# Residues of the matmul operands' addresses, spread over a 512-byte period, in a two-layer decoder trunk

## The chip, the cores and the metric

The kernel runs on one core of a Trainium2 chip. The metric is the device time of one execution in microseconds (us); less is better. A core has a tensor engine (PE, whose loads of the stationary operand are listed as PEld), a vector engine (DVE), a scalar engine (ACT), GpSimd (POOL) and a queue engine (SP) that starts DMAs. Operands of PE lie in the on-chip memory SBUF, 128 partitions wide; an address below is a byte offset within a partition, and its *residue* is the remainder after division by 512.

## The reference

256 tokens of width 2048 go through one layer of gated linear attention (GLA, 4 heads) and one layer of retention (8 heads), each with a SiLU gate path, and a last RMSNorm. All is float32.

```python
h = x
h = h + gla_mixer(rms_norm(h, gla_norm[0]), gla_w_in[0], gla_w_a1[0], gla_w_a2[0], gla_b_a[0], gla_head_g[0], gla_w_out[0])
h = h + retention_mixer(rms_norm(h, ret_norm[0]), positions, ret_w_in[0], ret_gn_g[0], ret_gn_b[0], ret_w_out[0])
return rms_norm(h, final_norm)
# a mixer, in short
q, k, v, gate = split(h @ w_in)                  # widths 1024/1024/4096/4096 in GLA, 2048/2048/4096/4096 in retention
o = per_head_norm(chunked_attention(q, k, v))    # with decays, scores masked causally
return (o * silu(gate)) @ w_out                  # 4096 -> 2048
```

## The kernel before

**Precision by parts.** A float32 number x is split into `hi`, what PE's "r" format of 32 bits keeps of it, and `lo` = x - `hi`. A product of tokens and weights is then three matmuls that add up in one PSUM bank: token-high by weight-hi, token-high by weight-lo, token-low by weight-hi (`mm3`, L341 to L343, and `three`, L412 to L414). The q and k projections take two and a half: the weight is the loaded operand there, 256 columns of high and 256 of low tokens stream past `hi` at once (L372, L382, L384), and the high tokens alone past `lo` (L374, L381, L385).

**Weights.** They come from HBM in pieces of 512 KB (two k-tiles of 128 rows by 512 columns, [128, 1024] in SBUF) into eight `raw` buffers, and a few into two spare ones. `emit_split` (L284 on) splits a piece: ACT copies `raw` to `hi` (L298), DVE subtracts to `lo` (L299). Pools `hi` and `lo` have four buffers each; `split_tiles` hands out a pair. `next_weights` splits up to three pieces (LOOK) ahead of the matmuls. The last pieces' `hi` parts lie in the tokens' tile, which is free by then. Some pieces are sums of two weight blocks, formed by accumulating DMAs and DVE adds (L293), for a scheme that saves matmuls by combining blocks of tokens and of weights (`pair`, `values_and_gates`, `out_pair`; the sums of tokens are the tiles `sums`, `xsum`, `osum`, `rsum`).

**Tokens.** `xhl` holds the normalised tokens, transposed: 16 k-tiles of [128, 2, 256], the 2 being high and low part. `ogt` holds the gated outputs of half the heads in the same form, for the output projection. Both are filled by ACT and DVE (L500, L501, L546, L549, L714, L715) and read by PE for most of the run: a k-tile's 128 tokens as the loaded operand against weight parts, or 512 columns of a k-tile as the streamed operand in the q and k groups. `make_sums` reads them for the sums of tokens (L448).

**Addresses.** Tiles of the pool `one` are placed one behind the other in the order of the `const` calls (rounded up to 32 bytes), and the pools `rs`, `raw`, `hi`, `lo` and the others behind them. `xhl` begins at 5,120, `ogt` at 37,888, and each `hi` and `lo` buffer at a multiple of 4,096 plus 1,024: all of residue 0, as are all k-tiles, their halves, and the two 512-column parts of a weight piece. A few small operands lie elsewhere: `ones_r` (loaded in L776) at 73,888, and the 48-column slices of `wa1` (loaded in L640) at a distance of 192 bytes.

**Order.** The work of one head (scores, norms, gate, transposes) is cut into steps of generators, `side` and `tasks`, which `advance` and `step` run between the matmuls of the next group; the framework's scheduler then orders each engine's instructions, and `keep` pins some. For every matmul PE gets a load of its stationary operand and the matmul itself; loads run while the matmul before them streams.

Of the kernel before, what the change touches and what calls it, by code (L numbers as in the profile page):

```python
# [11 lines left out]
F32R = mybir.dt.float32r  # L12
# [5 lines left out]
P = 128  # L18
SEQ = 256
D = 2048  # L20
EPS = 1e-6
NKT = D // P
GW = 512
SUB = 2
# [154 lines left out]
def kernel(  # L179
# [23 lines left out]
    hi_p = pool("hi", 4)  # L203
    lo_p = pool("lo", 4)
# [16 lines left out]
    def const(shape, name, dtype=F32):  # L221
        return one.tile(shape, dtype, tag=name, name=name)
# [51 lines left out]

    def split_tiles(i):
        if i < last0:
            hi = hi_p.tile([P, SUB, GW], F32R, tag="hi", name=f"hi{i}")
            lo = lo_p.tile([P, SUB, GW], F32R, tag="lo", name=f"lo{i}")
            return hi, lo
        j = i - last0  # L280
        hi = xhl[:, j * SUB : (j + 1) * SUB].rearrange("p k a t -> p k (a t)")
        return hi, t4_p.tile([P, SUB, GW], F32R, tag="t4", name=f"tail{j}")

    def emit_split(pieces=1, between=None):  # L284
        i = emitted["sub"]
        c, pre, post = subs[i]
        emit_raws(c)
        src = raws[c]
        for n in range(i + 1, min(i + 1 + EARLY, len(subs))):
            at, by = subs[n][:2]  # L290
            if by is not None and n not in added:
                added.add(n)
                nc.vector.tensor_tensor(raws[at], raws[at], raws[by], ALU.add)  # L293
        hi, lo = split_tiles(i)
        step = SUB // pieces
        for k in range(pieces):
            sl = slice(k * step, (k + 1) * step)
            a = nc.scalar.activation(hi[:, sl], src[:, sl], AF.Copy)  # L298
            b = nc.vector.tensor_tensor(lo[:, sl], src[:, sl], hi[:, sl].bitcast(F32), ALU.subtract)  # L299
            if i >= last0 - 4:  # L300
                keep(a)
                keep(b)
            if i == 0:
                first(a, b)
                if k == 0:
                    between()
        splits[i] = (hi, lo)
        emitted["sub"] += 1
        for n, key in post:
            nc.gpsimd.dma_start(raws[n], block(key), accum_op=ALU.add)  # L310
        emit_raws(c)
# [193 lines left out]
    sm = const([P, 96], "smalls")[:, 0:S_N]  # L505
    ident = const([P, P], "ident")
    cur["resid"] = rs_p.tile([P, 2, D], F32, tag="rs", name="resid")
    xhl = const([P, NKT, 2, SEQ], "xhl", F32R)
    ogt = const([P, NKT, 2, SEQ], "ogt", F32R)
    trig = const([P, 2, SEQ], "trig")  # L510
    rr = const([P, 2, 2], "rr")
    r2_ = const([P, 2, 2], "r2")
# [1075 lines left out]
```

## Time and profile before

| | before |
|---|---|
| median of 2 runs | 1374.33 us (1373.35 to 1375.31) |
| profiled execution: span from first to last instruction | 1371.5 us |
| PE busy, matmuls | 1362.3 us, 99%, 6,564 |
| DVE busy | 1098.4 us, 80% |
| ACT busy | 847.0 us, 62% |
| HBM read and written | 303.35 MB and 10.49 MB, 229 GB/s |
| mean granted clock of PE | 0.999 |

A profile is of one execution. A row of a group gives the kernel's line, the engine, the operation, the tile written and the tiles read, the size, the count; then the busy time in us, the mean duration of one in ns, and the engine's idle time just before, with what ended it. A row of the chain gives the start in us from the span's start, how long the piece held the chain, and what it was. A row of waits gives who waited for whom, the us in total, how often, and the longest. A row of the busy times of a stretch gives the stretch, its length, then busy us and count for PE, PEld, DVE and ACT, then the granted clock, the share of DMA time and GB/s. Matmuls overlap, so a matmul's duration (some 390 ns for 512 columns) is longer than the distance between two.

### The profile page before, as it was taken

The page shows a single profiled execution, that of the slowest core. Times are in us where ns is not written, and L with a number is a line of the kernel's source. Part 1 is how long each engine was busy: PE and PEld are TensorE (multiplying, and loading weights), DVE is VectorE, ACT ScalarE, POOL GpSimd, SP SyncE. Part 2 cuts the span into 40 slices and gives each one's busy share as a digit, 9 for nine tenths or more (in the row PEclk, how much of TensorE's full clock was granted, in tenths as well). Part 3 has the DMA queues.
Part 4 walks back from the last instruction along what each step waited for, and adds up shares of the span by engine and source line. Part 5 has one row for each costly group of instructions (what it writes and reads, how often), then busy time and mean ns, then how long its engine had stood idle before and what let it go on. Part 6 is the DMA issues. An engine that isn't in the chain of part 4 may idle for free.

```text
span 1371.5 us, 18372 instructions
## 1 busy us (share of the span) xinstructions
PE 1362.3 (99%) x6564; PEld 1145.0 (83%) x6564; DVE 1098.4 (80%) x1520; ACT 847.0 (62%) x1119; POOL 136.8 (10%) x194
## 2 busy tenths in 40 slices
PE   9999999999999999999999999999999999999997
PEld 8888888888888888888888888888888888888886
DVE  6686795987878896769887988897867897889796
ACT  6576656656567756656666576655546665666565
POOL 1003020110021021001011010100101101010010
PEclk9999999999999999999999999999999999999999
DMA  9755566789658667868897878796798797979773
GB/s 358 259 175 168 169 208 184 156 247 318 200 153 262 204 204 183 319 169 232 267 331 197 260 202 249 207 316 218 172 367 219 240 261 197 259 198 317 241 176 124
DMA packets 84508, 315.04 MB, mean 230 GB/s; under 512 B 9776, under 2 KB 10800, under 8 KB 83136
## 3 DMA queue, kind: packets, MB, share of 16 engines
q1 hardware_dynamic: 67200, 241.63, 50.4%
q0 software_dynamic: 15920, 64.89, 23.9%
q10 hardware_dynamic: 1296, 7.35, 1.4%
q8 instruction: 51, 0.84, 0.2%
q14 instruction: 41, 0.34, 0.1%
HBM read 303.35 MB, written 10.49 MB: 229 GB/s over the span
## 4 chain that ended last, share of the span: by engine, by line
PE 99%; DMA 1%; DVE 0%; ACT 0%; DVEq 0%; issue 0%; ACTq 0%
PE rqk_ps L384 8%; PE re_ps L412 8%; PE re_ps L413 8%; PE re_ps L414 8%; PE rqk_ps L385 4%; PE gqk_ps L384 4%; PE gg_ps L342 3%; PE gv_ps L343 3%; PE gv_ps L341 3%; PE gv_ps L342 3%; PE gg_ps L341 3%; PE gg_ps L343 3%; PE ge_ps L412 2%; PE ge_ps L413 2%; PE ge_ps L414 2%; PE gae_ps L413 2%
## 5 line engine op out<-in xcount | busy, mean ns | idle before, releaser
L299 DVE TENSOR_TENSOR lo<-raw,hi 128x1024 fp32r<-128x1024 f32 (+1 forms) x568 | 687.4, 1221 | 215.5 <-ACT hi L298 205.5
L298 ACT ACTIVATE hi<-raw 128x1024 fp32r<-128x1024 f32 (+1 forms) x568 | 595.9, 1055 | 394.3 <-DMA raw<-in_w_all 50.8
L384 PE MATMUL rqk_ps<-xhl,hi 128*128 128x512 f32 x480 | 162.9, 397 | 0.0
L413 PE MATMUL re_ps<-lo,xhl 128*128 128x512 f32 x352 | 137.5, 391 | 0.0
L414 PE MATMUL re_ps<-hi,xhl 128*128 128x512 f32 x352 | 137.3, 390 | 0.0
L310 POOL DMA_DIRECT2D raw<-in_w_all x90 | 78.0, 868 | 556.1 <-DVE lo L299 222.1
L412 PE MATMUL re_ps<-hi,xhl 128*128 128x512 f32 x352 | 132.6, 391 | 0.0
L385 PE MATMUL rqk_ps<-xhl,lo 128*128 128x256 f32 x480 | 122.5, 281 | 0.0
L384 PEld LDWEIGHTS rqk_ps<-xhl,hi 128*128 128x128 f32 x480 | 89.7, 188 | 17.8
L385 PEld LDWEIGHTS rqk_ps<-xhl,lo 128*128 128x128 f32 x480 | 87.6, 189 | 3.4
L414 PEld LDWEIGHTS re_ps<-hi,xhl 128*128 128x128 f32 x352 | 66.1, 188 | 13.6
L413 PEld LDWEIGHTS re_ps<-lo,xhl 128*128 128x128 f32 x352 | 66.2, 188 | 13.2
L412 PEld LDWEIGHTS re_ps<-hi,xhl 128*128 128x128 f32 x352 | 66.0, 188 | 13.2
L384 PE MATMUL gqk_ps<-xhl,hi 128*128 128x512 f32 x216 | 76.6, 399 | 0.0
L342 PE MATMUL gg_ps<-lo,xhl 128*128 128x512 f32 x192 | 75.5, 393 | 0.0
L342 PE MATMUL gv_ps<-lo,xhl 128*128 128x512 f32 x192 | 75.3, 392 | 0.0
L341 PE MATMUL gv_ps<-hi,xhl 128*128 128x512 f32 x192 | 75.2, 393 | 0.0
L343 PE MATMUL gv_ps<-hi,xhl 128*128 128x512 f32 x192 | 75.1, 391 | 0.0
L343 PE MATMUL gg_ps<-hi,xhl 128*128 128x512 f32 x192 | 75.0, 391 | 0.0
L341 PE MATMUL gg_ps<-hi,xhl 128*128 128x512 f32 x192 | 74.9, 392 | 0.0
L829 POOL TENSOR_TENSOR s<-s,m 128x64 f32<-128x64 f32 x56 | 36.1, 676 | 232.5 <-DVE m L820 223.2
L385 PE MATMUL gqk_ps<-xhl,lo 128*128 128x256 f32 x216 | 59.1, 281 | 0.0
(434 smaller groups left out, 2659.8 us busy)
## 6 DMA issues: line engine op xcount, KB each, us to landing
raw<-in_w_all SPq DMA_DIRECT2D x449, 512.0 KB, 4.9
raw<-in_w_all POOLq DMA_DIRECT2D x90, 512.0 KB, 6.8
resid<-in_x_n SPq DMA_DIRECT2D x2, 1024.0 KB, 10.8
gg<-in_gn_g POOLq DMA_DIRECT2D x8, 256.0 KB, 4.2
resid_x<-resid ACTq DMA_DIRECT2D x1, 2048.0 KB, 7.9
gb<-in_gn_b POOLq DMA_DIRECT2D x8, 256.0 KB, 6.0
gb_resid<-resid_x POOLq DMA_DIRECT2D x1, 2048.0 KB, 11.3
resid_g<-gb_resid ACTq DMA_DIRECT2D x1, 2048.0 KB, 10.5
```

Of the source, the lines that this page charges most:

```text
L298: a = nc.scalar.activation(hi[:, sl], src[:, sl], AF.Copy)
L299: b = nc.vector.tensor_tensor(lo[:, sl], src[:, sl], hi[:, sl].bitcast(F32), ALU.subtract)
L310: nc.gpsimd.dma_start(raws[n], block(key), accum_op=ALU.add)
L341: pin(mm(ps, xh, hi[:, q, :], start=kt == 0, stop=False, **onto))
L342: pin(mm(ps, xh, lo[:, q, :], start=False, stop=False, **onto))
L343: pin(mm(ps, xl, hi[:, q, :], start=False, stop=kt == end - 1, **onto))
L384: mm(ps[c], wh, rhs[:, kt, :, :], start=kt == 0, stop=False)
L385: mm(ps[c][:, 0, :], wl, rhs[:, kt, 0, :], start=False, stop=False)
L412: pin(mm(ps, xh, hi[:, q, :], start=start, stop=False, **again))
L413: pin(mm(ps, xh, lo[:, q, :], start=False, stop=False, **again))
L414: pin(mm(ps, xl, hi[:, q, :], start=False, stop=stop, **again))
L829: nc.gpsimd.tensor_tensor(dst, dst, side_of(m[:, li, :], z), ALU.add)
```

## The change

Each buffer of `hi` and `lo` becomes 64 bytes longer (16 floats), so the four buffers of a pool begin 64 bytes further on in residue each. A k-tile of `xhl` becomes 16 bytes longer and one of `ogt` 32 bytes, and an unused tile of 256 bytes stands between the two. The views that the rest of the kernel sees have the shapes of before.

```diff
     def split_tiles(i):
         if i < last0:
-            hi = hi_p.tile([P, SUB, GW], F32R, tag="hi", name=f"hi{i}")
-            lo = lo_p.tile([P, SUB, GW], F32R, tag="lo", name=f"lo{i}")
-            return hi, lo
+            both = []
+            for p, tag in ((hi_p, "hi"), (lo_p, "lo")):
+                t = p.tile([P, SUB * GW + 16], F32R, tag=tag, name=f"{tag}{i}")
+                both.append(t[:, 0 : SUB * GW].rearrange("p (k n) -> p k n", n=GW))
+            return both
...
-    xhl = const([P, NKT, 2, SEQ], "xhl", F32R)
-    ogt = const([P, NKT, 2, SEQ], "ogt", F32R)
+    rows = lambda t: t[:, :, 0 : 2 * SEQ].rearrange("p k (a t) -> p k a t", a=2)
+    xhl = rows(const([P, NKT, 2 * SEQ + 4], "xhl", F32R))
+    const([P, 64], "gap")
+    ogt = rows(const([P, NKT, 2 * SEQ + 8], "ogt", F32R))
```

## The prediction

> **What bounds the kernel now.** I read the page first (its busy times, its slices, its chain), then the waits of PE, then the chain in order of time for single stretches, then the groups by form, and last the busy times of the whole span for one tile at a time.
>
> ```profile
> span 1371.5 us, 18372 instructions
> PE 1362.3 (99%) x6564; PEld 1145.0 (83%) x6564; DVE 1098.4 (80%) x1520; ACT 847.0 (62%) x1119; POOL 136.8 (10%) x194
> DVE  6686795987878896769887988897867897889796
> PEclk9999999999999999999999999999999999999999
> PE 99%; DMA 1%; DVE 0%; ACT 0%; DVEq 0%; issue 0%; ACTq 0%
> PE warm_ps L521 <- POOL lnone L523: 1.0, 1, 1.0
> PE zps L640 <- DVE wa L614: 0.4, 1, 0.4
> ```
>
> The chain that ended last is 99% PE, the granted clock is full in every slice, and the whole list of what PE waited for is the last two rows: 1.4 us. So the time is 6,564 matmuls one behind the other, some 208 ns apart on average, plus about 9 us of start and end. DVE and ACT cost nothing while the weights they split arrive in time, and the two rows say that they do. The change moves addresses and nothing else, so what matters is the distance from the start of one matmul to the start of the next, which I call a step. The chain in order of time gives it, because each piece there lasts until the next begins (a matmul's own duration doesn't: they overlap).
>
> ```profile
> 716.87 0.23 PE re_ps L413
> ...
> 718.91 0.23 PE re_ps L414
> ...
> 746.43 0.91 PE rqk_ps L384 x4
> 747.34 0.47 PE rqk_ps L385 x4
> 747.81 0.23 PE rqk_ps L384
> 748.05 0.12 PE rqk_ps L385
> ...
> 749.23 0.94 PE rqk_ps L384 x4
> ```
>
> From the first to the second row lie nine steps of 512 columns in 2.04 us: 226.7 ns each. Four steps of 512 columns take 0.91 us (227.5 ns each), four of 256 columns 0.47 us (117.5 ns). The difference, 110 ns for 256 columns, makes 220 ns for 512; the remaining 7.5 ns of a step are there whatever its length. This remainder, not the columns, is what an address could change. The last rows show that steps can be worse: between 747.81 and 749.23 lie four pairs of 512 and 256 columns in 1.42 us, 355 ns a pair, where the calm rows add up to 345, so 5 ns more for each step; and 0.94 us for four steps is 235 ns each, 7.5 more than the calm ones.
>
> **The change part by part.** Today every large operand of PE begins at a multiple of 512 bytes: weight parts are 4,096 bytes, a k-tile of tokens is 2,048, a half of it 1,024. Afterwards the four `hi` buffers begin at 0, 64, 128 and 192 past a multiple of 512, the four `lo` buffers at 256 to 448, the k-tiles of `xhl` at 0 to 240 in steps of 16, those of `ogt` at 0 to 480 in steps of 32. No instruction, DMA, wait or queue position is added or removed: the new tile `gap` is never read or written, and the slack of 256 bytes in `xhl`, 512 in `ogt`, 512 in the weight parts and the gap of 256 only shift what lies behind by multiples of 512. The order of the work is planned from durations into which no address enters, so I take it as it is. The `raw` buffers, where the weights land, keep their residue, so the DMAs keep their time. How many steps are touched is in the busy times of the whole span for the tiles `xhl`, `ogt`, `hi` and `lo`, in this order:
>
> ```profile
> 0.00:1372.00 1372.00, 877.70 (x4072) 707.33 (x4072) 23.90 (x42) 17.40 (x35) 1.00 0.76 230
> 0.00:1372.00 1372.00, 291.50 (x1260) 232.56 (x1260) 35.12 (x56) 22.95 (x48) 1.00 0.76 230
> 0.00:1372.00 1372.00, 1170.44 (x3688) 689.60 (x3688) 687.44 (x568) 595.95 (x568) 1.00 0.76 230
> 0.00:1372.00 1372.00, 761.40 (x2228) 415.32 (x2228) 687.44 (x568) 1.00 0.76 230
> ```
>
> A matmul that reads `hi` or `lo` is one of 5,916. In the q and k groups the weight part is what is loaded and the tokens stream past it (L384, L385 and their kin, about 1,550 steps counting the low-rank gate's); in all others tokens, gated outputs or their sums are loaded and the weight part streams (some 4,400 steps). With the few others that stream 32-bit "r" values the count of steps that could change is about 6,200.
>
> *The operand that is loaded* (about 5,250 loads of `xhl`, `ogt`, `hi` and `lo`). Some loads in this trace already begin elsewhere: `ones_r` of L776 lies 160 bytes past a multiple of 512 (the constants before it add up to that), and the 48 columns of `wa1` that L640 loads lie 192 bytes apart, so they take all eight multiples of 64.
>
> ```profile
> L384 PEld LDWEIGHTS rqk_ps<-xhl,hi 128*128 128x128 f32 x480 | 89.7, 188 | 17.8
> L776 PEld LDWEIGHTS dg<-qkp,ones_r 128*128 128x128 f32 x16 | 2.7, 188 | 0.5
> L640 PEld LDWEIGHTS zps<-xhl,wa 128*48 128x48 f32 x16 | 1.9, 122 | 1.3 <-DVE wa L614 0.6
> L667 PEld LDWEIGHTS rb<-dg,ones 128*16 128x16 f32 x4 | 0.3, 95 | 0.4 <-issue 0.4
> 81.51 0.35 PE dg L776 x3
> 12.05 1.12 PE zps L640 x4
> 16.19 0.69 PE zps L640 x3
> ```
>
> A load of 128 columns takes 188 ns from either address. 16 columns take 95, so 112 more cost 93, and 48 columns should take 122: measured 122 at the mixed residues. The steps around these loads are ordinary too: three of 256 columns in 0.35 us are 117 ns each (calm: 117.5), three of 512 columns 230. The first four L640 steps, in the unsteady start, have 280. I take nothing for this term. What hides a longer load is the idle time ahead of each: 17.8 us over 480 loads, 37 ns; a load would have to grow by a fifth before a 512-column step felt it. Under a 256-column step no such cover is seen, and a load longer by 7.5 ns there would cost 800 x 7.5 = 6 us. Multiples of 16 that are no multiples of 32, as half of `xhl` will have, no row shows.
>
> *The weight part that streams*, 4,400 steps at multiples of 64: no row shows a stream that begins off a multiple of 512. Its bounds are those of the remainder: at best all of it goes, minus 7.5 ns a step, minus 33 us; at worst each step takes the bad form above, plus 7.5 ns, plus 33 us. Between them I take 0, by the row that is nearest, the loads at multiples of 64, which read the same memory and cost nothing extra.
>
> *The tokens that stream*, 1,550 steps, 15 of 16 of them off their old residue, half of these at odd multiples of 16: bounds plus and minus 7.5 ns, 12 us. [...]
>
> *ACT and DVE* write and read these tiles at shifted addresses: 564 splits on each.
>
> ```profile
> L299 DVE TENSOR_TENSOR lo<-raw,hi 128x1024 fp32r<-128x1024 f32 x564 | 684.8, 1224 | 214.4 <-ACT hi L298 204.4 <-DMA raw<-in_w_all 3.8
> L801 DVE TENSOR_TENSOR w<-w,qk 128x256 f32<-128x256 f32 x28 | 11.8, 422 | 0.1
> L802 DVE TENSOR_TENSOR w<-w,qk 128x256 f32<-128x256 f32 x28 | 11.8, 422 | 0.0
> L748 DVE TENSOR_TENSOR lc<-lc 128x256 f32<-128x256 f32 x4 | 1.7, 422 | 0.0
> ACT hi L298 <- PE gg_ps L343: 49.0, 28, 3.0
> ```
>
> L801 and L802 start at offsets of 4 to 256 bytes, by level, and take 422 ns as does L748 at an aligned address: no cost on DVE. The cover is in the last row and its like: the splits wait for PE to give a buffer back, so they run ahead.
>
> The sum: 0 + 0 + 3 us. The profiled execution spans 1371.5 us, which would become 1374.5; the runs of before have a median of 1374.33, 2.8 more than the span for what lies around it. So the forecast is 1374.3 + 3 = **1377 us**, with a range of its own of 1365 to 1392.
>
> **The rivals.** *Faster: the remainder is a collision.* Each load starts right as a matmul starts, and today both begin at the same residue. If the 7.5 ns are the two reads meeting in one place of the memory, most pairs of residues would lose them: 6,564 x 7.5 = 49 us, a time of 1325; with half the pairs freed 1350. For it speaks that the remainder is the same for 256 and 512 columns, as something at the start of a step would be. Against it speak L776 and L640, whose loads already begin at another residue than the stream over which they run, with steps of 117 and 230 ns. The Trainium skill, on the page "TensorE: Matmul & The Clock Gate" (section "Back-to-back issue gap"), gives N / 2.4 + 2.5 ns for a warm step, 216 ns for 512 columns; the rows here have 227, so by that page 11 ns of each step are something else, and losing them would save about 70 us rather than 49, as an estimate from that page. The same page's section on issuing a matmul says that stationary and moving operand have read ports of their own and take no bandwidth from each other, which would leave nothing to save; the rows of L776 and L640 side with that.
>
> *Slower: the streams meet halfway.* Today load and stream run in a fixed phase. With shifted residues they may cross in mid-stream, and every crossing would stop the columns. The price is that of the bad steps which the trace has already: 5 to 7.5 ns on 6,200 steps, 31 to 47 us, so 1405 to 1421, say 1415. Its place is every stage alike, the stretches of weights streaming past `xhl` above all. It decides from 4.4 ns a step on average (27.5 us over 6,200). For it: such steps exist, and the pattern of alternating 512 and 256 columns has them most. Against it: the same two residue tests, which show none.
>
> *Slower: the splits.* If shifted destinations slowed ACT or DVE, PE would begin to wait for `hi` and `lo` where DVE has no room: nine slices of 34 us show a 9. A split longer by 8% would take 9 x 34 x 0.08 = 25 us there, a time of 1400. The rows of L801 and L802 speak against it.
>
> *The change does nothing measurable*, 1374 us, if residues in steps of 16 bytes are all one to PE. That is inside the forecast's own range.
>
> **How the numbers follow.** The forecast with its own range, 0.57: two independent tests on loads show no residue, and none on streams exists. The faster rival by over 2% (below 1347), 0.17; the crossing, over 1402, 0.22; the splits, 0.04. A change of 2%, 27.5 us, is about what a measurement of this kernel can tell from no change. So faster 0.17, same 0.57, slower 0.26. The range for 8 in 10 runs from 1335, which holds most of the faster rival's span (1325 to 1347), to 1425, just above the crossing's upper price.
>
> **What would show it.** In the changed profile the calm steps should still be 0.91 us for four L384 steps and 2.04 us for nine steps of L412 to L414, loads 188 ns, the split 1,224 ns, and PE's list of waits under 3 us. Steps of L384 grouped by k-tile of `xhl` should differ by 0 to 4 ns between k-tile 0 and the odd ones. The forecast is wrong if the steps of weights streaming past tokens leave 225 to 229 ns on average: near 220 the collision is right, at 232 or more the crossing. It is wrong in another way if PE's waits rise by tens of microseconds behind `hi` or `lo`.

## The result and the profile after

The changed kernel takes **1394.77 us** (median of 2 runs, 1394.74 to 1394.80) where the kernel before takes 1374.33: a ratio of 1.0152, with a 95% interval of 1.0135 to 1.0169. It is 20 us slower: less than 2%, but the interval lies clear of 1. Added lines move the line numbers of the profile by 2: L384 to L386, L412 to L414 up to L414 to L416, L299 to L301; behind the allocation of `xhl`, where two more are added, by 4 (L521 to L525).

From the page of the changed kernel: span, busy times, slices, chain; then the list of what PE waited for, and the groups by form.

```profile
span 1392.9 us, 18372 instructions
PE 1384.1 (99%) x6564; PEld 1145.5 (82%) x6564; DVE 1099.7 (79%) x1520; ACT 847.5 (61%) x1119; POOL 137.0 (10%) x194
PEclk9999999999999999999999999999999999999999
PE 99%; DVE 0%; ACT 0%; DVEq 0%; issue 0%; POOL 0%; POOLq 0%
```

```profile
PE warm_ps L525 <- POOL lnone L527: 1.0, 1, 1.0
```

```profile
L301 DVE TENSOR_TENSOR lo<-raw,hi 128x1024 fp32r<-128x1024 f32 x564 | 685.2, 1224 | 233.0 <-ACT hi L300 223.6 <-DMA raw<-in_w_all 4.9 <-PE rqk_ps L387 1.4
L386 PEld LDWEIGHTS rqk_ps<-xhl,hi 128*128 128x128 f32 x480 | 89.5, 188 | 18.0
```

Everything that a usual search would look at is as before: the same instructions, the full clock, 1.0 us of waits on PE, splits of 1,224 ns, loads of 188 ns. PE's busy time alone has grown, by the 21.4 us by which the span has grown. So the steps are longer. The chain in order of time shows it at the same nine matmuls as before:

```profile
727.95 0.93 PE rqk_ps L386 x4
728.88 0.23 PE re_ps L415
...
730.97 0.23 PE re_ps L416
```

Nine steps now take 2.09 us, 232 ns each, instead of 2.04 (226.7 ns). A longer stretch of one kind, where weights stream for 265 steps of 512 columns and gated outputs of `ogt` are loaded (in 48 of the steps their sums), gives it more exactly. The rows are the busy times of that stretch, before and then after (its length in us stands second; the loads in it, 265, count the steps):

```profile
945.45:1005.52 60.07, 60.07 (x266) 49.77 (x265) 46.92 (x48) 33.49 (x34) 5.22 (x6) 1.00 0.75 214
```

```profile
960.34:1021.91 61.57, 61.57 (x266) 49.75 (x265) 47.07 (x48) 33.36 (x34) 5.24 (x6) 1.00 0.73 209
```

60.07 us for 265 steps are 226.7 ns each, 61.57 us are 232.3. The time of the loads hardly moves (49.77 and 49.75 us). In the longest stretch of q and k, where tokens stream and weights are loaded (127 steps), nothing is lost, 22.35 us before and 22.20 after:

```profile
1009.15:1031.50 22.35, 22.35 (x128) 19.44 (x127) 11.07 (x12) 9.51 (x11) 2.27 (x3) 1.00 0.98 348
```

```profile
1025.63:1047.83 22.20, 22.20 (x128) 19.44 (x127) 11.00 (x12) 9.52 (x11) 2.28 (x3) 1.00 0.98 345
```

Adding up the distances from start to start over the whole trace, by what is loaded and what streams, accounts for all of it:

| steps | count | before, us | after, us | ns a step |
|---|---|---|---|---|
| weights stream past `xhl` | 2,472 | 564.7 | 576.4 | 228.4 to 233.2 |
| weights stream past `ogt` | 1,196 | 273.2 | 279.4 | 228.4 to 233.6 |
| weights stream past sums of tokens | 720 | 164.3 | 167.3 | 228.3 to 232.3 |
| tokens stream past weights, 512 columns | 768 | 181.0 | 180.3 | 235.7 to 234.8 |
| tokens stream past weights, 256 columns | 768 | 90.4 | 90.9 | 117.8 to 118.4 |
| all 6,563 steps | | 1362.4 | 1383.8 | |

Of the 21.4 us, 20.9 lie in the 4,388 steps in which a weight part streams.

### The profile page after: what moved, and what is told of

The parts are those of the page before. It is cut to its first block, busy times and chain, and to the rows that moved or that the text cites. A ratio compares the mean times of both kernels' runs of the same rounds, so it can differ in the third digit from the quotient of the medians.

```text
span 1392.9 us, 18372 instructions
## 1 busy us (share of the span) xinstructions
PE 1384.1 (99%) x6564; PEld 1145.5 (82%) x6564; DVE 1099.7 (79%) x1520; ACT 847.5 (61%) x1119; POOL 137.0 (10%) x194
## 4 chain that ended last, share of the span: by engine, by line
PE 99%; DVE 0%; ACT 0%; DVEq 0%; issue 0%; POOL 0%; POOLq 0%
PE rqk_ps L386 8%; PE re_ps L414 8%; PE re_ps L415 8%; PE re_ps L416 8%; PE rqk_ps L387 4%; PE gqk_ps L386 4%; PE gg_ps L344 3%; PE gv_ps L343 3%; PE gg_ps L343 3%; PE gv_ps L345 3%; PE gg_ps L345 3%; PE gv_ps L344 3%; PE ge_ps L414 2%; PE ge_ps L416 2%; PE ge_ps L415 2%; PE gae_ps L416 2%
## 5 line engine op out<-in xcount | busy, mean ns | idle before, releaser
L301 DVE TENSOR_TENSOR lo<-raw,hi 128x1024 fp32r<-128x1024 f32 (+1 forms) x568 | 687.9, 1221 | 233.1 <-ACT hi L300 223.6
L386 PE MATMUL rqk_ps<-xhl,hi 128*128 128x512 f32 x480 | 163.2, 396 | 0.0
L416 PE MATMUL re_ps<-hi,xhl 128*128 128x512 f32 x352 | 138.6, 394 | 0.0
L414 PE MATMUL re_ps<-hi,xhl 128*128 128x512 f32 x352 | 133.9, 395 | 0.0
L386 PEld LDWEIGHTS rqk_ps<-xhl,hi 128*128 128x128 f32 x480 | 89.5, 188 | 18.0
L416 PEld LDWEIGHTS re_ps<-hi,xhl 128*128 128x128 f32 x352 | 66.2, 188 | 15.2
L414 PEld LDWEIGHTS re_ps<-hi,xhl 128*128 128x128 f32 x352 | 66.0, 188 | 14.8
L386 PE MATMUL gqk_ps<-xhl,hi 128*128 128x512 f32 x216 | 76.5, 396 | 0.0
L833 POOL TENSOR_TENSOR s<-s,m 128x64 f32<-128x64 f32 x56 | 36.0, 676 | 236.5 <-DVE m L824 226.6
```

What stands on the lines that cost most here:

```text
L386: mm(ps[c], wh, rhs[:, kt, :, :], start=kt == 0, stop=False)
L414: pin(mm(ps, xh, hi[:, q, :], start=start, stop=False, **again))
L416: pin(mm(ps, xl, hi[:, q, :], start=False, stop=stop, **again))
L833: nc.gpsimd.tensor_tensor(dst, dst, side_of(m[:, li, :], z), ALU.add)
```

## The experiments

Four theories were held against each other. **Alignment**: an operand that begins off a multiple of 512 bytes costs by itself, as stream or as load. **Place**: some absolute place in memory is worse than others. **Distance**: what counts is how far the address of the operand being loaded for the next matmul lies from that of the operand now streaming. **Succession**: any fixed distance is harmless, and a step loses time only when the addresses differ from those of the step before. The expectations call Distance the offset theory, and a later form of Succession the settling theory. "Distance" below is the start address of the loaded operand minus that of the streamed one, modulo 256 where it is compared. The settled step is the mean from the eleventh step of a stretch on. The order of the matmuls is the same in all these kernels.

### Either half of the change alone

*Weights alone*: `split_tiles` of the changed kernel, with `xhl` and `ogt` as before.

```diff
-            hi = hi_p.tile([P, SUB, GW], F32R, tag="hi", name=f"hi{i}")
-            lo = lo_p.tile([P, SUB, GW], F32R, tag="lo", name=f"lo{i}")
...
+                t = p.tile([P, SUB * GW + 16], F32R, tag=tag, name=f"{tag}{i}")
...
```

> The weight parts alone lie 64 bytes apart; xhl and ogt are as before. Succession theory (a step costs its short time only while each matmul's addresses have the residues of the one before; every change of residue unsettles the steps that follow): the streamed residue changes at nearly every matmul, so the whole loss, 1392 to 1396 us. Offset theory (what costs is the distance between the residues of the loaded and of the streamed operand): 7 of 8 pairs are apart, 1391 to 1395 us. Alignment theory (the tokens' odd multiples of 16 cost): no loss, 1373 to 1376 us.

Measured: 1391.58 us against 1373.96, ratio 1.0123 (1.0108 to 1.0138).

*Tokens alone*: the slack of `xhl` and `ogt` and the gap, with weight buffers as before.

```diff
-    xhl = const([P, NKT, 2, SEQ], "xhl", F32R)
...
+    xhl = rows(const([P, NKT, 2 * SEQ + 4], "xhl", F32R))
+    const([P, 64], "gap")
+    ogt = rows(const([P, NKT, 2 * SEQ + 8], "ogt", F32R))
```

> The slack of xhl and ogt and the gap alone; weight parts are as before. Succession theory: the tokens' residue changes only from k-tile to k-tile, every 3 to 6 matmuls, and as loaded operand in most groups; if loaded residues count as streamed ones do, 1385 to 1393 us, if only the streamed operand counts 1374 to 1378 us. Offset theory: 15 of 16 pairs are apart, 1392 to 1396 us. Alignment theory: the whole loss, 1392 to 1396 us.

Measured: 1392.76 us against 1373.96, ratio 1.0132 (1.0117 to 1.0148). The 265-step stretch, weights alone and then tokens alone:

```profile
957.71:1018.99 61.28, 61.28 (x266) 49.75 (x265) 47.05 (x48) 33.35 (x34) 5.24 (x6) 1.00 0.74 210
```

```profile
958.78:1020.45 61.67, 61.67 (x267) 49.69 (x265) 46.84 (x48) 33.36 (x34) 5.24 (x6) 1.00 0.73 208
```

Steps of 231.2 and 232.7 ns. Each half alone costs nearly as much as both, 17.6 and 18.8 us of 20.4. Costs that belonged to single operands and to each of them would add up; these don't. In the second kernel the weights stream from their old residue and the steps are longer all the same, and in the first the tokens have lost nothing of their alignment. So it seems that the two operands must meet. In the narrow form of the expectations (odd multiples of 16 in the tokens) Alignment is out by the first kernel. In the wide form it isn't yet: a cost that is paid once, whichever operand is off, would not add up either. The kernel with everything at residue 64, below, decides that. Distance had both times inside its ranges; Succession had the tokens' time inside and missed the weights' by 0.4 us.

### Everything moved, and distances held fixed

*The whole behind the tokens moved by 1,536 bytes*: no residue modulo 512 changes.

```diff
+    const([P, 384], "gap")
```

> An unused tile of 1,536 bytes ahead of trig moves raw, hi, lo and all tiles behind them by three times 512, so no residue modulo 512 changes, but all distances modulo 1,024, 2,048 and 4,096 between tokens and weights do. Succession, offset and alignment theory with a period of 512: no loss, 1373 to 1376 us. A theory of absolute places, or of a longer period: a loss of up to 20 us.

Measured: 1373.73 us against 1373.96, ratio 0.9995 (0.9985 to 1.0005).

*Everything at residue 64*: a tile of 64 bytes ahead of `xhl` moves tokens and weights together, so that the distance stays 0.

```diff
+    const([P, 16], "gap")
     xhl = const([P, NKT, 2, SEQ], "xhl", F32R)
```

> An unused tile of 64 bytes ahead of xhl: tokens, gated outputs, sums and weight parts all lie at residue 64, so every distance between loaded and streamed residue is 0 as before. If the distance alone counts: 1372 to 1376 us, settled steps 226.7 ns. If the absolute residue counts (64 was among the changed ones): 1385 to 1396 us.

Measured: 1373.52 us against 1373.44, ratio 0.9998 (0.9989 to 1.0007).

*Weights at a fixed 64*: two unused tiles put every `hi` and `lo` buffer at residue 64, tokens at 0, so the distance is the same in nearly every step. Where tokens are loaded and weights stream, it is minus 64, which is 192 modulo 256; it is 64 in the q and k groups.

```diff
+    hi_p.tile([P, 16], F32, tag="pad", name="pad_hi_p", bufs=1)
+    v_p.tile([P, 112], F32, tag="pad", name="pad_v_p", bufs=1)
```

> All eight weight buffers at residue 64, everything else at residue 0 as before: one constant distance of 64 bytes between the loaded and the streamed operand. Succession theory: nothing changes from matmul to matmul, 1372 to 1377 us, steps of 512 columns settle to one value. Offset theory: the whole loss or more, 1390 to 1398 us. Alignment theory: no loss.

Measured: 1385.30 us against 1373.96, ratio 1.0076 (1.0061 to 1.0091). That is outside all three ranges, between Succession's and Distance's.

*`lo` at 256, `hi` at 0*: distances alternate between 0 and 256 from matmul to matmul.

```diff
+    lo_p.tile([P, 64], F32, tag="pad", name="pad_lo_p", bufs=1)
+    v_p.tile([P, 64], F32, tag="pad", name="pad_v_p", bufs=1)
```

> All hi buffers at residue 0, all lo buffers at 256, tokens at 0. Each operand keeps its residue, but the streamed one alternates between hi and lo. Settling theory (steps of unchanged residues settle into a short cycle, whose mean depends on the distance between loaded and streamed residue; any change of either unsettles them to some 232 ns): if only a change counts, alternation never settles, about 1390 us; if a regular alternation may settle too, a cycle of three steps with a mean between 225 and 231 ns, 1366 to 1388 us. Rival, any distance other than 0 costs the same 2 ns or more: one step of three is at distance 256, 1377 to 1382 us.

Measured: 1373.37 us against 1373.38, ratio 1.0002 (0.9992 to 1.0012). The 265-step stretch of the four kernels in the order told:

```profile
945.99:1006.06 60.07, 60.07 (x266) 49.75 (x265) 46.89 (x48) 33.47 (x34) 5.24 (x6) 1.00 0.76 213
```

```profile
946.00:1006.08 60.08, 60.08 (x267) 49.76 (x266) 46.90 (x48) 33.48 (x34) 5.23 (x6) 1.00 0.74 215
```

```profile
953.07:1013.73 60.66, 60.66 (x267) 49.77 (x265) 47.01 (x48) 33.47 (x34) 5.24 (x6) 1.00 0.76 212
```

```profile
945.39:1005.47 60.08, 60.08 (x266) 49.75 (x265) 46.90 (x48) 33.37 (x34) 5.23 (x6) 1.00 0.76 213
```

The second row takes place and alignment away together: with all operands off their old residue by 64 bytes the steps are 226.7 ns, as before. The third is against succession as the whole cause: nothing changes from step to step, and yet each takes 228.9 ns. It is also less than the 232.3 of the changed kernel, so a constant distance of this size isn't the whole loss either. The fourth says that a distance of 256 bytes is as good as 0. Since it is, this kernel doesn't test what a change between unequal distances costs. What is left is the distance, modulo 256 bytes, with a part of succession still open.

### The price of each distance

Three kernels measure it. `xhl` and `ogt` get rooms that are 512 bytes longer, and each filling of them begins at an offset of its own; weights stay at residue 0.

```diff
+    XAT, OAT = (16, 32), (64, 128, 256, 384)
+    xhl_room = const([P, NKT * 2 * SEQ + 128], "xhl", F32R)
+    ogt_room = const([P, NKT * 2 * SEQ + 128], "ogt", F32R)
...
+    xhl, ogt = room_at(xhl_room, XAT[0]), room_at(ogt_room, OAT[0])
...
+    ogt = room_at(ogt_room, OAT[1])
```

The second has 96 and 480 for `xhl` and 48, 192, 320, 144 for `ogt`, the third 240 and 112, and 80, 160, 176, 208.

> Weights at residue 0; xhl lies 16 bytes on in the first layer and 32 in the second, ogt 64, 128, 256 and 384 bytes on in its four fillings. Six constant distances in one run, each for 300 to 1,400 steps. Settling theory: in each of the six stretches the 512-column steps settle within some ten steps to a cycle of their own, with means that differ between 222 and 232 ns. Rival, any distance other than 0 costs the same: 229 ns in all six. Total 1370 to 1395 us either way.

Measured: 1388.08 us against 1373.38, ratio 1.0107 (1.0087 to 1.0128). The rival's one price of 229 ns falls by the rows below; the means reach 233.3, just over the 232 expected.

> As before with other distances: xhl 96 and 480, ogt 48, 192, 320 and 144 bytes. Settling theory: six means again, equal to those of the other run where the distance is the same modulo the period. Rival: 229 ns in all six. Total 1370 to 1395 us.

Measured: 1395.95 us against 1373.38, ratio 1.0165 (1.0144 to 1.0185), 1 us above the range.

> The six distances that are missing: xhl 240 and 112 bytes on, ogt 80, 160, 176 and 208. With them all 16 multiples of 16 modulo 256 are measured. If distance explains the loss, the mean of the 16 settled steps lies within 1 ns of the 232.1 ns of the changed kernel (231 to 233) and the six lie between 226.7 and 235 ns; if it is the change from matmul to matmul, the mean of the settled steps is 229 ns or less.

Measured: 1388.50 us against 1373.44, ratio 1.0106 (1.0088 to 1.0125).

Settled stretches of one distance each. First kernel: 16 (107 steps), 16 again (78), 64 (70), 256 (115), 384 (58):

```profile
34.77:59.03 24.26, 24.26 (x109) 20.08 (x107) 15.13 (x30) 15.52 (x27) 0.00 (x0) 1.00 0.78 273
508.64:526.84 18.20, 18.20 (x80) 14.74 (x78) 9.71 (x11) 9.93 (x11) 4.88 (x9) 1.00 0.75 197
...
282.71:299.04 16.33, 16.33 (x71) 13.16 (x70) 12.57 (x13) 8.50 (x8) 1.72 (x2) 1.00 0.99 284
956.19:982.25 26.06, 26.06 (x116) 21.59 (x115) 17.57 (x19) 13.73 (x15) 1.78 (x2) 1.00 0.66 181
1296.00:1309.53 13.53, 13.53 (x59) 10.89 (x58) 11.29 (x25) 5.51 (x7) 1.10 (x2) 1.00 0.70 211
```

That is 226.7, 233.3, 233.3, 226.6 and 233.3 ns a step. Second kernel: 96 (84 steps), 144 (58), 144 again (67), 320 (58):

```profile
217.98:237.66 19.68, 19.68 (x86) 15.82 (x85) 11.75 (x12) 10.26 (x13) 0.00 (x0) 1.00 0.57 168
1306.07:1319.22 13.15, 13.15 (x59) 10.89 (x58) 11.31 (x25) 5.58 (x7) 1.10 (x2) 1.00 0.68 216
1323.58:1339.21 15.63, 15.63 (x69) 12.58 (x67) 12.99 (x16) 10.47 (x15) 2.35 (x3) 1.00 0.70 164
...
946.18:959.71 13.53, 13.53 (x60) 10.90 (x58) 11.30 (x25) 5.51 (x7) 1.08 (x2) 1.00 0.71 216
```

That is 234.3, 226.7, 233.3 and 233.3. Third kernel: 176 (115 steps) and 240 (84):

```profile
955.03:981.48 26.45, 26.45 (x117) 21.57 (x115) 17.59 (x19) 13.73 (x15) 1.78 (x2) 1.00 0.65 178
213.77:232.81 19.04, 19.04 (x86) 15.77 (x84) 11.73 (x12) 10.33 (x13) 0.00 (x0) 1.00 0.59 182
```

That is 230.0 and 226.7. All settled steps of these three, of the kernel before and of the one with weights at 64, from their start times in the traces, by distance modulo 256 (in ns; a star where one stretch had 226.7 and another some 233):

| 0 | 16 | 32 | 48 | 64 | 80 | 96 | 112 |
|---|---|---|---|---|---|---|---|
| 226.7 | 230.0* | 233.3 | 233.3 | 233.3 | 232.1 | 234.3 | 233.3 |

| 128 | 144 | 160 | 176 | 192 | 208 | 224 | 240 |
|---|---|---|---|---|---|---|---|
| 232.5 | 229.0* | 233.4 | 230.0 | 229.2 | 232.3 | 233.3 | 227.1 |

The price does not grow with the distance; only 0 is free throughout, and 240 nearly so. The mean of all 16 is 231.4 ns, 4.8 over the free one and inside the 231 to 233 that the last expectation asked for if distance explains the loss. On average it sizes the change: with the distances that each settled step of the changed kernel has, the table gives 231.35, and measured is 232.11. Of the 5.4 ns above 226.7 the table thus accounts for 4.65 (86%). The two half changes leave about the same rest: by the table 230.4 and 230.7, measured 231.3 and 231.6.

This is a match of means only. Sorted by distance, the settled steps of the changed kernel lie between 230.4 and 233.6 ns, where the table goes from 226.7 to 234.3: at distance 0 they take 231.1 instead of 226.7, at 64 they take 232.3 instead of 233.3. So where the distance changes from step to step, a step doesn't pay the price of its own distance. A rival stays untested here: steps whose distance keeps changing may take some 232 ns whatever the distances are. A kernel that alternates between two cheap distances which differ modulo 256, 0 and 240 say, would tell; none was run. What is shown is that unequal residues cost this much on average even where nothing changes.

### A version that beats both

In the q and k groups a matmul of 512 columns and one of 256 alternate for much of the time. Settled pairs of them took some 350.5 ns at distance 0 in the kernel before, and some 347 at 224 and 240 in the first of the three kernels above. So q and k weights were put 32 bytes below the others modulo 256, and all others left at distance 0 or 256. Two constants were also shortened, which moves tokens, sums and weights together by 64 bytes modulo 256; the same move cost nothing with everything at residue 64. The lines that place the weights:

```diff
+            o = 56 if loads[subs[i][0]][0][0] in ("aqk", "rqk") else 0
...
+                t = p.tile([P, SUB * GW + 64], F32R, tag=tag, name=f"{tag}{i}")
+                both.append(t[:, o : o + SUB * GW].rearrange("p (k n) -> p k n", n=GW))
```

> Weight parts of the q and k groups lie 224 bytes further on than all other weight parts (modulo 256 that is 32 back), so the loaded operand of those groups stands at distance 224 from the streamed tokens, everywhere else the distance stays 0. Settling theory with the pair means seen at distances 224 and 240 (347 ns for 512 and 256 columns together, against 350.5 at 0): 768 pairs x 3.5 = 2.7 us less, 1370 to 1373 us. Rival, the shorter pairs at those distances were due to something else in that run: 1373 to 1378 us, as weights of two residues follow each other in the mixed stretches.

Measured: 1372.01 us against 1373.44, ratio 0.9987 (0.9978 to 0.9996). The 265 steps and the 127 steps of q and k:

```profile
944.22:1004.29 60.07, 60.07 (x266) 49.74 (x265) 46.88 (x48) 33.43 (x34) 5.23 (x6) 1.00 0.75 214
1007.94:1029.91 21.97, 21.97 (x129) 19.47 (x127) 11.02 (x12) 9.52 (x11) 2.28 (x3) 1.00 0.97 351
```

The calm steps stay at 226.7 ns and the q and k stretch falls from 22.35 to 21.97 us. The gain of 1.4 us is small, but the interval of its ratio lies below 1. It is half of the 2.7 us expected, which priced all 768 pairs as settled ones. The two kinds of step moved against each other: over the whole trace the 768 steps of 512 columns fall from 235.7 to 231.7 ns, and the 768 of 256 columns rise from 117.8 to 119.7, 1.55 us less in all.

## Why the prediction was right, and where it was wrong

The forecast of 1377 us was 18 us too low, and its own range of 1365 to 1392 was missed by 2.8 us. The wide range of 1335 to 1425 and the call of less than 2% held, and both by luck: the wide range had been drawn to cover the rivals, and the time fell into the gap between the forecast's own range and the 1402 us from which the crossing would have counted as slower. Nor is 2% what a measurement of this kernel can tell: 1.5% is clear of no change here (1.0135 to 1.0169).

- *The bound of the kernel* was read rightly: PE's steps set the time, before and after, and the 21.4 us of the span are the 21.4 us of the steps.
- *The weight part that streams*, taken at 0 with bounds of 7.5 ns either way, is **the term that failed**: 4,388 steps grew by 4.1 to 5.2 ns, 20.9 us in all. "By the row that is nearest, the loads at multiples of 64" was the wrong neighbour: the loads take 188 ns on average in every one of the kernels, at any distance, and the time is lost between the starts of the matmuls over which they run.
- *The operand that is loaded*, at 0, fails with it: neither half can be priced alone, since the sum of two zeros left out the pair. The test on L640 was also misread. Its three steps in 0.69 us are 230 ns, 3.3 above the calm 226.7, and the prediction called that ordinary. L776 could tell nothing, for its three steps have 256 columns, which hardly lose: 117.8 to 118.4 ns on average over the 768 such steps of q and k.
- *The tokens that stream*, plus 3 us in the sum: no run shows this term; measured is minus 0.2 us (the two rows of the table). The sign and the size were a guess, and it was the only term the forecast had. The test stated for it, 0 to 4 ns between k-tile 0 and the odd ones, tells nothing: the L386 steps have 233.2 and 234.6 ns, but the same steps of the kernel before have 232.2 and 236.2.
- *ACT and DVE*, 0: right. The split took 1,224 ns before and takes 1,224 now, and PE's waits went from 1.4 to 1.0 us.
- *"The streams meet halfway"* was right on what meets (the load and the stream), on the sign, and on the place ("the stretches of weights streaming past `xhl` above all"); that the two cross in mid-stream is not shown. Its price was too high: 6,200 steps were charged where only some 4,400 pay, so 1405 to 1421 became 1395, and over its 6,200 steps the loss is 3.4 ns, under the 4.4 from which it was to decide. Charged by its own 5 to 7.5 ns, 4,388 steps would have given 22 to 33 us; the measured 4.8 lies just below. The bad steps that it took the price from are no sign of a crossing, for in the kernel before all of these operands lie at distance 0: 355 ns a pair was held against 345 from unmixed rows, while settled pairs there take some 350.5, and steps just behind a disturbance are longer too (last section).
- *"The remainder is a collision"* falls as priced. Equal residues are the best of the sixteen distances for a calm step, so the 7.5 ns that steps of any length share are not the two reads meeting at one residue. The rule of the Trainium skill that the prediction set beside it, from the page "TensorE: Matmul & The Clock Gate" (section "Part 2: What happens when you issue a matmul"), is that the stationary and the moving operand have read ports of their own and that loading takes nothing from the stream. The 188 ns of the loads agree; the steps do not, as settled ones range from 226.7 to 234.3 ns when only the distance is changed, and the measurement decides.
- *The test stated in advance* decided as written: the forecast is wrong if steps of weights past tokens leave 225 to 229 ns on average, and 232 or more meant the crossing. They are 232 in the chain, 232.3 in the long stretch, and 233.2 over all steps past `xhl`.

What stays open is the mechanism inside. That the distance between the two operands makes the steps longer is shown by moving either one, both together, and each by many amounts; how much of the changed kernel's loss is the distances and how much their changing stays open too, as only the means match. Why the period is 256 bytes, why 96 is worst, and what stops the stream, no view of the trace tells.

## What to carry to other kernels

Where a kernel is a row of matmuls with a new load each, as here (128 columns loaded, 512 streamed, 32-bit "r" values), keep the start addresses of the loaded and the streamed operands equal modulo 256 bytes; spreading the residues cost 1.5% here. Other shapes and types were not run, and pairs of 512 and 256 columns did a little better at 224. Measure a step as a long stretch's length over its count, and let no row count as calm that lies 1 to 2% above the calm one. When two operands are in use at once, price the pair, not each by itself.

## What the runs showed of the hardware that was not expected

**Settling.** In the kernel before, 512-column steps that follow shorter matmuls begin at 235 ns on average, take 230.7 as the fourth and 227.4 as the tenth, and then stay at 226.7. The chain in order of time shows it behind the transposes that come just before the 265 steps of 226.7:

```profile
943.90 0.55 PE rot_tp L707 x5
944.45 0.23 PE ra_ps L341
...
946.07 0.23 PE ra_ps L342
```

The first seven steps take 1.62 us, 231.4 ns each. In the changed kernel the mean stays between 230.9 and 232.6 ns at every position behind shorter matmuls: it never settles. Even its steps at distance 0, which occur among others, take 231.1 ns.

**Two states of one distance.** At distances of 16 and 144 the same kernel has stretches of 226.7 and of 233.3 ns, steady for 58 steps and more, as the rows above show. Other distances do it too: 240 has 226.7 and 228.4, and the kernel with all weights at 64 has, beside its 228.9, stretches of 233.3 at the same distance of 192. One of them, 40 steps past `xhl`:

```profile
917.38:926.71 9.33, 9.33 (x41) 7.56 (x40) 9.33 (x13) 6.21 (x8) 0.56 (x1) 1.00 0.90 344
```

So the distance alone doesn't fix the step, and some entries of the table are means over two states. What decides between them is not known.
